# Single-core hybrid decoder layer: x blocks in rested places and loads untied, zeros on TensorE ahead of the first data, a residual sum between two side products, late forms' sums ten ticks on

## The chip, the core and the metric

The kernel runs on one core of a Trainium2 chip. The core has TensorE (PE, matmuls), VectorE (DVE), ScalarE (ACT), GpSimd (POOL) and SyncE (SP); SP and POOL issue the loads and stores, each from a queue of its own that is worked off in order. Each engine also runs its instructions in the order in which they stand in its own list, and waits at the first whose input is missing. The metric is the time of one execution in microseconds of device time.

## The reference

One layer on 512 tokens with 2048 columns, all in float32:

```python
h    = rmsnorm(x, attn_norm_g);  proj = h @ w_in          # 9216 columns: u, v, q, k, v_att, g_a, g_b
y_a  = chunked spatial gating of u, v                      # 8 groups, chunks of 128
y_b  = stick-breaking attention of q, k, v_att             # 8 heads of 128, strictly causal
x    = x + (sigmoid(g_a) * (y_a @ w_up_a) + sigmoid(g_b) * (y_b @ w_up_b)) @ w_o
hid  = rmsnorm(x, ffn_norm_g) @ w_ffn_in                   # 2 x 5632 columns, gate and up
x    = x + (silu(gate) * up) @ w_ffn_out
x    = x + sigmoid(rmsnorm(x, ple_norm_g) @ w_ple_gate) * (p @ w_ple)   # p: 512 x 256
```

## The kernel before

Everything lies transposed: columns on the 128 partitions, the 512 tokens along the free axis. x is eight blocks of 256 columns, each 128 x 1024 numbers. A float32 matrix is split into a high part that TensorE takes at its fast float32 rate and the rest (`split_into`: ACT writes the high part, DVE subtracts it), and a product is three matmuls: high by high, high by low, low by high (`mm3`, lines L268 to L270). Most products are done by Strassen's scheme on pairs of blocks: seven products in place of eight, of sums of the four quarters of each operand ("S" forms, L659); the rest are plain ("P"). What is prepared of an activation block is called a form: the gain of the norm by ACT (`gained`, L499), four sums by DVE (L512), and the splits (L263 by ACT, L264 by DVE). Weights go through three steps: they land in `wholes`, DVE adds sums (L363), ACT makes `whi` (L347), DVE makes `wlo` (L344); there are three places for `whi` and `wlo`. A finished unit is brought together by DVE from the PSUM banks (L702, L705).

Two arenas hold it all: `parts` for forms and `wholes`, 13200 columns for what lands. A place is taken "low" (the lowest hole), "high", "tight" (the smallest hole) or "rested" (the place that has been free longest). A place that is taken again makes the next load wait until everything that read it is done. Beside them there are two wide buffers, `out`, handed out in turn.

The program is traced by a planner. A counter, `clock`, ticks once per product of a pair of forms. At each tick the next form in the list `builds` goes a step on if its places fit (`fits`), up to three forms ahead may fetch their raw block early, and postponed steps that are due are put in. The instructions that a tick adds are kept behind the products already issued. Loads of weights and x are held in the order in which the code wrote them by `in_order`.

*The head.* The side product p @ w_ple comes in eight pairs of columns (`ple_pair`): the first three are done at the very start while x arrives, each ending in an ACT copy from PSUM to `out` (L830) and a store. Then the first three units of w_in are made plainly, block by block of x, while x arrives; their weights are `w_first`. `x_form(k)` loads x up to block k + 2, applies the gain, adds the block's squares to the first norm (`Norm.add`: ACT squares L901, DVE sums L905) and splits it.

*The end of w_o.* The product with w_o goes through eight blocks j; each ends with the residual's sum (`pr.onto`, L757) and its squares for the second norm. After the products of the last block `ple_pair` 3 and 4 stand ahead of that sum, 5, 6 and 7 after. The norm then sums squares over partitions by TensorE (L914), takes the power, builds four diagonal blocks on DVE (`diagonals`, L888) and spreads the row over the partitions with four matmuls of these diagonals (L930).

*The FFN.* 43 hidden units from w_ffn_in, whose results are stored to memory ("hid", 22 blocks); then w_ffn_out in three passes over the hidden blocks, the first two with five S forms ahead of three or two plain ones. S forms of hidden blocks and of x2 are `late_form`: they fetch the raw block early, and do their four sums in `plain_first` when they are built, ahead of the splits.

## Time and profile before

| | us |
|---|---|
| three runs, median | 2719.37 (2715.48 to 2728.74) |
| the profiled execution, its own time | 2723.71 |
| its span (first to last instruction) | 2721.8 |
| mean granted TensorE clock | 0.995 |
| PE busy | 2670.8 (98% of the span) |
| DVE busy | 2166.5 (80%) |
| ACT busy | 1357.0 (50%) |
| POOL busy | 392.8 (14%) |

In the chain of work that ended last, PE has 84%, DVE 6%, DMA 4%, ACT 3%. A row of a timeline below reads: start in us, duration in us, engine, line, operation, output <- input, and in brackets the engine's idle time ahead of it with what ended it. A row of the stages: the stretch, its length, and for each engine its busy time with the number of instructions, then the granted clock, the mean share of the DMA engines and what they moved in GB/s. Line numbers in the profile are those of the kernel before; the rows of the order after carry the changed kernel's own numbers.

### The profile page before, as it was taken

Reading aid. Unit: us, or ns where it says so; the run is one execution under the profiler, and the core shown is the slowest. Engines: PE = TensorE matmul, PEld = TensorE weight load, DVE = VectorE, ACT = ScalarE, POOL = GpSimd, SP = SyncE. Lnnn points to the kernel's source line nnn. Section 1 sums busy time; section 2 is a strip of 40 time slices with the busy share of each in tenths; the row PEclk is TensorE's granted clock in tenths of the full one; section 3 lists DMA queues with packets and bytes.
Section 4 is the critical chain, followed back from the end, with each engine's and each line's share of the span. In section 5 each row is a group of like instructions: output and inputs, shape, how many; then the busy total and the mean of one; then the engine's idle time right before and its main releaser. Section 6 shows DMA issues by size and latency. Waiting matters only on the chain.

```text
span 2721.8 us, 43177 instructions
## 1 busy us (share of the span) xinstructions
PE 2670.8 (98%) x15907; PEld 2358.2 (87%) x15907; DVE 2166.5 (80%) x3715; ACT 1357.0 (50%) x2143; POOL 392.8 (14%) x439
## 2 busy tenths in 40 slices
PE   6999999999999999999999999999999999999999
PEld 5888888888888889988888888888888998989898
DVE  6687878788888657678989898989899567688876
ACT  6565656564555334365444444444445344454543
POOL 0112121211220000001111111111110111101110
PEclk8999999999999999999999999999999999999999
DMA  5667677777776447667888888788886668788784
GB/s 175 165 169 181 177 178 178 175 182 193 175 182 220 135 137 223 196 200 188 209 221 201 208 197 207 200 204 202 203 203 194 171 175 247 203 250 233 253 223 135
DMA packets 303412, 528.88 MB, mean 194 GB/s; under 512 B 25696, under 2 KB 162912, under 8 KB 303200
## 3 DMA queue, kind: packets, MB, share of 16 engines
q1 hardware_dynamic: 242448, 425.70, 49.1%
q0 software_dynamic: 60752, 100.43, 23.1%
q8 instruction: 125, 2.05, 0.3%
q14 instruction: 87, 0.71, 0.1%
HBM read 478.84 MB, written 47.19 MB: 193 GB/s over the span
## 4 chain that ended last, share of the span: by engine, by line
PE 84%; DVE 6%; DMA 4%; ACT 3%; issue 2%; POOL 0%; SPq 0%; DVEq 0%; ACTq 0%; POOLq 0%
PE ps L659 38%; PE ps L268 13%; PE ps L270 13%; PE ps L269 13%; PE small L659 4%; DVE wlo L344 2%; ACT whi L347 1%; DMA wholes<-w_in 1%; DVE parts L264 1%; DVE wholes L512 1%; DVE out L705 1%; DVE wholes L705 1%; PE small L1090 1%; PE small L1048 1%; DVE wholes L363 1%
## 5 line engine op out<-in xcount | busy, mean ns | idle before, releaser
L347 ACT ACTIVATE whi<-wholes 128x512 fp32r<-128x512 f32 (+4 forms) x950 | 846.9, 916 | 845.2 <-DVE wholes L363 286.4
L659 PE MATMUL ps<-parts,whi 128*128 128x512 f32 x3384 | 1127.1, 397 | 3.0 <-DVE p L705 1.9
L344 DVE TENSOR_TENSOR wlo<-wholes,whi 128x512 fp32r<-128x512 f32 (+4 forms) x950 | 961.6, 1044 | 97.5 <-ACT whi L347 96.5
L268 PE MATMUL ps<-parts,whi 128*128 128x256 f32 (+1 forms) x2675 | 857.3, 323 | 28.6 <-ACT whi L347 23.1
L269 PE MATMUL ps<-parts,whi 128*128 128x256 f32 (+1 forms) x2640 | 856.3, 324 | 0.9 <-DVE parts L264 0.9
L270 PE MATMUL ps<-parts,wlo 128*128 128x256 f32 (+1 forms) x2640 | 854.9, 324 | 1.8 <-DVE wlo L344 1.8
L659 PEld LDWEIGHTS ps<-parts,wlo 128*128 128x128 f32 x3384 | 634.9, 188 | 141.0
L659 PE MATMUL ps<-parts,wlo 128*128 128x256 f32 x3384 | 667.5, 278 | 0.0
L268 PEld LDWEIGHTS ps<-parts,whi 128*128 128x128 f32 x2675 | 509.5, 191 | 75.0 <-ACT whi L347 25.2
L659 PEld LDWEIGHTS ps<-parts,whi 128*128 128x128 f32 x3384 | 542.7, 189 | 10.2 <-issue 3.9
L269 PEld LDWEIGHTS ps<-parts,whi 128*128 128x128 f32 x2640 | 502.9, 191 | 45.1 <-DVE parts L264 2.2
L270 PEld LDWEIGHTS ps<-parts,wlo 128*128 128x128 f32 x2640 | 502.8, 190 | 41.0 <-DVE wlo L344 2.4
L363 DVE TENSOR_TENSOR wholes<-wholes 128x256 f32<-128x256 f32 (+1 forms) x794 | 327.7, 413 | 21.1 <-DMA wholes<-w_ffn_out 3.0
L351 POOL DMA_DIRECT2D wholes<-w_ffn_in x172 | 149.7, 870 | 752.4 <-DVE wlo L344 219.2
L705 DVE TENSOR_TENSOR out<-out,ps 128x256 f32<-128x256 f32 x373 | 152.9, 420 | 127.4 <-ACT out L702 116.6
L351 POOL DMA_DIRECT2D wholes<-w_in x132 | 116.7, 884 | 637.9 <-DMA wholes<-w_in 294.2
L264 DVE TENSOR_TENSOR parts<-wholes,parts 128x1024 fp32r<-128x1024 f32 (+3 forms) x129 | 122.4, 962 | 19.1 <-ACT parts L263 18.9
L659 PE MATMUL small<-parts,whi 128*128 128x512 f32 x344 | 136.0, 395 | 0.0
L1359 ACT ACTIVATE out<-out 128x512 f32<-128x512 f32 x44 | 27.8, 632 | 195.2 <-DVE out L1358 195.2
L263 ACT ACTIVATE parts<-wholes 128x1024 fp32r<-128x1024 f32 (+3 forms) x129 | 105.8, 844 | 32.7 <-DMA wholes<-hid 11.1
L351 POOL DMA_DIRECT2D wholes<-w_ffn_out x56 | 56.9, 1015 | 397.9 <-DMA wholes<-w_ffn_out 146.4
L673 DVE TENSOR_TENSOR out<-out 128x256 f32<-128x256 f32 x36 | 15.3, 424 | 120.5 <-ACT out L670 120.5
(125 smaller groups left out, 1655.2 us busy)
## 6 DMA issues: line engine op xcount, KB each, us to landing
wholes<-w_ffn_in SPq DMA_DIRECT2D x172, 384.0 KB, 5.5
wholes<-w_in SPq DMA_DIRECT2D x132, 384.0 KB, 5.1
wholes<-w_ffn_in SPq DMA_DIRECT2D x172, 256.0 KB, 4.7
wholes<-w_ffn_in POOLq DMA_DIRECT2D x172, 256.0 KB, 5.2
wholes<-w_in SPq DMA_DIRECT2D x132, 256.0 KB, 4.1
wholes<-w_in POOLq DMA_DIRECT2D x132, 256.0 KB, 4.9
wholes<-x SPq DMA_DIRECT2D x32, 512.0 KB, 5.4
wholes<-w_ffn_out SPq DMA_DIRECT2D x31, 512.0 KB, 4.2
```

The source lines that it names most:

```text
L263: return (nc.scalar.activation(hi, src, AF.Copy), nc.vector.tensor_tensor(out=lo, in0=src, in1=hi.bitcast(F32), op=ALU.subtract))
L264: nc.vector.tensor_tensor(out=lo, in0=src, in1=hi.bitcast(F32), op=ALU.subtract))
L268: nc.tensor.matmul(ps[:, s], sh, mh[:, s], start=start, stop=False)
L269: nc.tensor.matmul(ps, sh, ml, start=False, stop=False)
L270: return nc.tensor.matmul(ps, sl, mh, start=False, stop=stop)
L344: in_turn(nc.vector.tensor_tensor(out=self.lo[:, blocks], in0=r, in1=h.bitcast(F32), op=ALU.subtract))
L347: in_turn(nc.scalar.activation(h, r, AF.Copy))
L351: nc.gpsimd.dma_start(out=raw[:, 3:5], in_=self.src[:, 1:3], accum_op=ALU.add)
L363: in_turn(nc.vector.tensor_tensor(out=o, in0=x, in1=y, op=ALU.add))
L659: i = nc.tensor.matmul(out, w, t, start=first and k == 0, stop=last and k == 1)
L705: in_turn(nc.vector.tensor_tensor(out=out, in0=x, in1=y, op=op))
L1359: nc.scalar.activation(g, g, AF.Silu)
```

## The change

- Ahead of everything five matmuls of zeros (128 x 256, float32) run on TensorE, into a bank that nobody reads. They need only a memset by DVE.
- p (`pT`) is loaded and split in two halves; its place is an ordinary one.
- The blocks of x are taken "rested" as far as the fourth (later ones "low"), so is the scaled copy in `x_form` as far as the third; `x_form(k)` loads up to block k, not k + 2. `in_order` is gone: loads of x and of weights have no order but that of SP's queue as the scheduler makes it.
- The three ple results of the head are stored by POOL's queue, later ones by SP's as before.
- At w_o's end the residual's sum stands between `ple_pair(3)` and `ple_pair(4)`.
- The second norm's row (and the others') is asked for two ticks later.
- A late form has its gain and its four sums done ahead of being built, ten ticks or more after its fetch (`sum_early`), if there is room for the sums and a spare block.
- How many spare blocks of 1024 columns that asks for (`spared`) is one, two from the start of the last pass, none once its last x1 block is loaded.

```diff
...
 PARTS = 16 * PLACE
 WHOLES = 13200
 FETCHED = 3
+WARM = 5
+LANDS = 10
 KEPT = 3
 HIDE = 2.0**99
 
...
             builds.popleft().step()
         for f in list(builds)[:FETCHED]:
             if f.fetches and f.early and f.ready():
-                if fits([(wholes, f.fetches, "low"), (wholes, 1024, "low")]):
+                if fits([(wholes, f.fetches, "low")] + spare_blocks()):
                     f.fetch()
                 break
+        any(f.sum_early() for f in list(builds)[:FETCHED])
         while waiting and waiting[0][0] <= clock[0]:
             heapq.heappop(waiting)[2]()
         for i in reversed(traced()):
...
                                          mybir.DependencyReason.DATA),
                     reason="in its place among the units")
 
+    spared = [1]
+
+    def spare_blocks():
+        return [(wholes, 1024, "low")] * spared[0]
+
     class Staged:
 
 
...
         spare[0] = sum(-1 for x in prepared if x.land.n < LANDING)
 
     chain = {}
-
-    def in_order(i):
-
-        if i.ins.engine in chain:
-            tc.add_manual_dep(
-                i.ins, chain[i.ins.engine],
-                mybir.DependencyInfo(mybir.DependencyClass.NoSync,
-                                     mybir.DependencyReason.DATA),
-                reason="in its place among the loads")
-        chain[i.ins.engine] = i.ins.name
 
     def in_turn(*instructions):
 
...
             landings.remove(self.land)
             raw = self.blocks(self.land.f())
             if kind == "P":
-                in_order(nc.sync.dma_start(out=raw, in_=src))
+                nc.sync.dma_start(out=raw, in_=src)
             else:
-                in_order(nc.sync.dma_start(out=raw[:, 3:5],
-                                           in_=src[:, 0:1].to_broadcast([P, 2, n * P])))
+                nc.sync.dma_start(out=raw[:, 3:5],
+                                  in_=src[:, 0:1].to_broadcast([P, 2, n * P]))
                 nc.sync.dma_start(out=raw[:, 0:3], in_=src[:, 1:4])
 
         def blocks(self, t, c=None):
...
             self.kind, self.places, self.ready = kind, sizes, ready
             self.blocks, self.at_plain, self.used = None, kind == "P", False
             self.src, self.fetches, self.raw, self.early = src, raw, None, False
+            self.late, self.gain, self.sums, self.since = False, None, None, None
 
         @property
         def sizes(self):
-            return self.places + [(wholes, self.fetches, "low")] * bool(self.fetches)
+            return (self.places + [(wholes, self.fetches, "low")] * bool(self.fetches)
+                    + SUMS * (self.late and self.sums is None))
 
         def fetch(self, block=None):
 
             if self.raw is None:
                 self.raw, self.fetches = block or self.src(), 0
+                self.since = clock[0]
             return self.raw
+
+        def scale(self):
+
+            if self.gain:
+                gained(self.raw.f(), self.raw.f(), *self.gain)
+                self.gain = None
+
+        def sum_early(self):
+
+            if not self.late or self.sums or self.since is None or clock[0] < self.since + LANDS:
+                return False
+            if self.gain:
+                self.scale()
+            elif fits(SUMS + spare_blocks()):
+                self.sums = sums_of(self.raw)
+            return True
 
         def get(self):
             if self in builds:
...
                                      AF.Copy, scale=gcol[:, gi + 2 * k + i : gi + 2 * k + i + 1])
                 for i in range(2)]
 
-    def plain_first(form, raw):
-
-
-        b, s, v = cut(raw.f()), take(768, "tight"), take(256, "tight")
-        t, x = cut(s.f()), form.operand()
+    SUMS = [(wholes, 768, "tight"), (wholes, 256, "tight")]
+
+    def sums_of(raw):
+
+        b, s, v = cut(raw.f()), *(take(n, how) for _, n, how in SUMS)
+        t = cut(s.f())
         for out, p, q, op in ((t[:, 0], b[:, 1], b[:, 0], ALU.subtract),
                               (v.f(), b[:, 1], b[:, 3], ALU.subtract),
                               (t[:, 1], t[:, 0], b[:, 3], ALU.subtract),
                               (t[:, 2], t[:, 1], b[:, 2], ALU.add)):
             nc.vector.tensor_tensor(out=out, in0=p, in1=q, op=op)
+        return s, v
+
+    def plain_first(form, raw):
+
+
+        s, v = form.sums or sums_of(raw)
+        b, t, x = cut(raw.f()), cut(s.f()), form.operand()
         split_into(x[:, 0:4, 0], x[:, 0:4, 1], b)
         give(raw)
         form.at_plain = True
...
         def steps(form):
             w = form.fetch()
             form.blocks = (parts.take(2 * PLACE, "place"),)
-            if gain:
-                gained(w.f(), w.f(), *gain)
-            yield
+            if not form.sums:
+                form.scale()
+                yield
             yield from plain_first(form, w)
             return form.operand()
 
-        return Form("S", steps, [(parts, 2 * PLACE, "place"), (wholes, 768, "tight"),
-                                 (wholes, 256, "tight")], ready, src, 1024)
+        f = Form("S", steps, [(parts, 2 * PLACE, "place")], ready, src, 1024)
+        f.late, f.gain = True, gain
+        return f
 
     def strassen_form(src, ready=always, gain=None, raw=PLACE):
 
...
     ps_p = []
 
     def ple_operands():
-        raw = load(pT)
+        raw = take(1024)
         hi, lo = parts.take(1024, "high"), parts.take(1024, "high")
-        split_into(hi.own(), lo.own(), raw.f())
+        for s in (slice(0, T), slice(T, 2 * T)):
+            nc.sync.dma_start(out=raw.f()[:, s], in_=pT[:, s])
+            split_into(hi.own()[:, s], lo.own()[:, s], raw.f()[:, s])
         give(raw)
         ps_p.extend((hi, lo))
 
...
                 mm3(ps, wh[:, s], wl[:, s], xh, xl, k == 0, k == 1)
             nc.scalar.activation(o[:, i * T : (i + 1) * T], ps, AF.Copy)
         d = tc.dram_tile([P, 1024], F32, name=nm("ple"))
-        nc.sync.dma_start(out=d, in_=o)
+        (nc.sync if planned else nc.gpsimd).dma_start(out=d, in_=o)
         ple_spill[j] = d
         slots.append(slot)
         tick()
...
     x_raw = []
 
     def load_x():
-        x_raw.append(take(1024))
-        in_order(nc.sync.dma_start(out=x_raw[-1].f(), in_=xT[len(x_raw) - 1]))
-
+        x_raw.append(take(1024, "rested" if len(x_raw) < KU - 4 else "low"))
+        nc.sync.dma_start(out=x_raw[-1].f(), in_=xT[len(x_raw) - 1])
+
+    idle, nothing = wide(), bank()
+    nc.vector.memset(idle[:, : T // 2], 0.0)
+    for _ in range(WARM):
+        nc.tensor.matmul(nothing[:, :T // 2], idle[:, :P], idle[:, :T // 2],
+                         start=True, stop=True)
     ple_operands()
     ple_pair(0, False)
     load_x()
...
             yield
             diags = diagonals(self.cols)
             yield
+            yield
+            yield
             ps = small_bank()
             for t in range(NT):
                 s = slice(t * P, (t + 1) * P)
...
 
     def x_form(k):
         def steps(form):
-            while len(x_raw) < min(k + 3, KU):
+            while len(x_raw) < min(k + 1, KU):
                 load_x()
             form.blocks = (parts.take(2 * PLACE, "place"),)
-            w = take(1024)
+            w = take(1024, "rested" if k < KU - 5 else "low")
             gained(w.f(), x_raw[k].f(), g_attn, k)
             norm1.add(x_raw[k])
             give(x_raw[k])
...
         pr = pair(ms, last=j == KU - 1)
         if j == KU - 1:
             ple_pair(3)
-            ple_pair(4)
         h = raw.popleft()
         pr.onto(h.f())
+        if j == KU - 1:
+            ple_pair(4)
         nc.sync.dma_start(out=spill["x1", j], in_=h.f())
         there.add(("x1", j))
         norm2.add(h)
...
         at += len(kinds)
         if c == len(PASSES) - 1:
             builds.extend(gs)
+            spared[0] = 2
         for j in range(KU):
             got = {}
 
             def fetch(*names, got=got, j=j):
                 for n in names:
                     got[n] = load(spill[n, j])
+                if "x1" in names and j == KU - 1:
+                    spared[0] = 0
 
             if c:
                 after(3, lambda f=fetch: f("sum"))
```

Three places show how it moves instructions. The first is SP's queue at the start: `pT` is p, `xT` a block of x, `ple` a stored side result, `w_first` the weights of the first three units. Before:

```order
L495 DMA wholes<-pT 128x1024
L327 DMA wholes<-w_ple 128x512
L853 DMA gcol<-gains 128x58
L847 DMA wholes<-xT 128x1024
L327 DMA wholes<-w_ple 128x512 x2
L327 DMA wholes<-w_first 128x512
L847 DMA wholes<-xT 128x1024
L832 DMA ple_107<-out_88 128x1024
L847 DMA wholes<-xT 128x1024
L832 DMA ple_158<-out_141 128x1024
L832 DMA ple_180<-out_163 128x1024
L847 DMA wholes<-xT 128x1024 x2
```

and with the change, the same queue from its first load:

```order
L841 DMA wholes<-pT 128x512 x2
L325 DMA wholes<-w_ple 128x512
L875 DMA wholes<-xT 128x1024
L886 DMA gcol<-gains 128x58
L325 DMA wholes<-w_ple 128x512 x2
L325 DMA wholes<-w_first 128x512
L875 DMA wholes<-xT 128x1024 x2
L325 DMA wholes<-w_first 128x512 x5
L327 DMA wholes<-w_in 128x2x256
```

The ple stores have left the queue; five blocks of x stood in it before the second group of `w_first` (the row after the last one above), now three, and the fourth comes after seven more loads of `w_first` and two of `w_in`.

The second place is ACT at the end of w_o. L830 (L858 with the change) is the copy of a ple result to `out`, L901 (L934) the Square of the last residual block into `out`, `whi` the weights' high part. Before:

```order
L347 ACTIVATE whi_76<-wholes 128x1024
L830 ACTIVATE out_10730<-ps_10731 128x512
L830 ACTIVATE out_10730<-ps_10739 128x512
L347 ACTIVATE whi_80<-wholes 128x1024
L901 ACTIVATE out_10759<-wholes 128x1024
L347 ACTIVATE whi_78<-wholes 128x1024
L830 ACTIVATE out_10766<-ps_10767 128x512
L830 ACTIVATE out_10766<-ps_10775 128x512
```

and with the change:

```order
L345 ACTIVATE whi_76<-wholes 128x1024
L858 ACTIVATE out_10747<-ps_10748 128x512
L858 ACTIVATE out_10747<-ps_10756 128x512
L934 ACTIVATE out_10773<-wholes 128x1024
L345 ACTIVATE whi_80<-wholes 128x1024
L271 ACTIVATE parts<-wholes 128x3x256
L858 ACTIVATE out_10780<-ps_10781 128x512
L858 ACTIVATE out_10780<-ps_10789 128x512
```

The two copies of ple 4 stay ahead; the Square has moved ahead of the next `whi`, and a split of a form has come in between. On PE, in the same stretch, the sums of squares over the partitions are row 6015 before and 6013 with the change, and the matmuls of the diagonals row 6073 before and 6086 with it. On DVE the last of the four diagonals then comes after a `wlo` of 128 x 1280.

The third place is DVE at the start of w_ffn_out's first pass. L512 (L530) are the sums of an S form, L264 (L272) its splits, L705 (L731) empties the PSUM banks of the last hidden unit. Before:

```order
L344 TENSOR_TENSOR wlo_79<-wholes,whi_78 128x1024
L512 TENSOR_TENSOR wholes<-wholes 128x256 x3
L264 TENSOR_TENSOR parts<-wholes,parts 128x4x256
L512 TENSOR_TENSOR wholes<-wholes 128x256 x4
L264 TENSOR_TENSOR parts<-wholes,parts 128x4x256
L512 TENSOR_TENSOR wholes<-wholes 128x256
L264 TENSOR_TENSOR parts<-wholes,parts 128x3x256
L512 TENSOR_TENSOR wholes<-wholes 128x256 x2
L264 TENSOR_TENSOR parts<-wholes,parts 128x4x256
L512 TENSOR_TENSOR wholes<-wholes 128x256
L264 TENSOR_TENSOR parts<-wholes,parts 128x3x256
L512 TENSOR_TENSOR wholes<-wholes 128x256
```

then the first L705; and with the change:

```order
L342 TENSOR_TENSOR wlo_79<-wholes,whi_78 128x1024
L272 TENSOR_TENSOR parts<-wholes,parts 128x4x256 x2
L272 TENSOR_TENSOR parts<-wholes,parts 128x3x256 x2
L530 TENSOR_TENSOR wholes<-wholes 128x256 x3
L272 TENSOR_TENSOR parts<-wholes,parts 128x4x256
L530 TENSOR_TENSOR wholes<-wholes 128x256
L731 TENSOR_TENSOR out_18713<-out_18713,ps_18588 128x256
```

Twelve sums stood ahead of the first L705 there; four do with the change. The other eight, of the first two hidden forms, now stand among the units of w_ffn_in.

## The prediction

> **What bounds the kernel now.** I read the page first (busy shares), then PE's waits, then a table by stage, and last the timelines of the places where PE stands still.
>
> ```profile
> span 2721.8 us, 43177 instructions
> PE 2670.8 (98%) x15907; PEld 2358.2 (87%) x15907; DVE 2166.5 (80%) x3715; ACT 1357.0 (50%) x2143; POOL 392.8 (14%) x439
> ```
> ```profile
> PE ps L268 <- ACT whi L347: 23.1, 6, 12.9
> PE small L930 <- DVE out L888: 4.6, 3, 2.3
> PE ps L268 <- ACT out L830: 2.8, 2, 1.5
> PE ps L268 <- DVE out L705: 2.4, 1, 2.4
> ```
> TensorE is the bound: 2721.8 - 2670.8 leaves 51.0 us in which it does nothing. The change adds or takes away no matmul of the layer, so all that can be won is those 51 us and the time in which PE runs at half speed. The waits (us in total, times, longest) say that one wait of 12.9 us is a quarter of the idle time. The stages say where the rest is:
>
> ```profile
> core 0: us, PE busy (x) PEld busy (x) DVE busy (x) ACT busy (x) POOL busy (x), PEclk, DMA share, GB/s
> 0.00:10.00 10.00, 3.93 (x9) 2.83 (x10) 2.14 (x5) 3.09 (x4) 0.95 (x7) 1.00 0.47 152
> 10.00:20.00 10.00, 8.86 (x37) 6.66 (x36) 3.69 (x6) 8.69 (x17) 0.00 (x0) 1.00 0.71 270
> 20.00:30.00 10.00, 1.15 (x6) 0.61 (x4) 8.96 (x18) 6.79 (x9) 0.00 (x0) 0.70 0.34 111
> 30.00:40.00 10.00, 5.94 (x19) 4.73 (x20) 8.82 (x15) 7.39 (x10) 0.00 (x0) 0.62 0.97 334
> 40.00:120.00 80.00, 75.25 (x365) 62.61 (x364) 49.56 (x89) 45.84 (x83) 8.46 (x9) 1.00 0.51 142
> ...
> 1235.00:2060.00 825.00, 825.00 (x4738) 719.85 (x4737) 743.53 (x1347) 390.62 (x553) 144.41 (x166) 1.00 0.82 204
> ```
> The first 120 us hold 24.9 us of PE's idle time, the end of w_o two more waits (2.3 on L888, 2.8 on L830), the start of ffn_out the one on L705; the FFN's first product, 1235 to 2060, has none. The change touches these three places with idle time and also the one without.
>
> **The head, part by part.** SP's queue and ACT, then PE:
>
> ```profile
> 6.78 0.33 SPq L847 DMA_DIRECT2D wholes<-xT  x1
> ...
> 25.55 3.51 SPq L847 DMA_DIRECT2D wholes<-xT  x2
> 29.12 1.37 SPq L327 DMA_DIRECT2D wholes<-w_first  x3
> ```
> ```profile
> 4.44 1.06 ACT L263 ACTIVATE parts<-wholes 128x1024 fp32r<-128x1024 f32 x1 [2.35 <-DMA wholes<-pT]
> ...
> 29.00 1.33 ACT L499 ACTIVATE wholes<-wholes,gcol 128x512 f32<-128x512 f32 x2 [3.18 <-DMA wholes<-xT]
> 30.24 1.04 ACT L901 ACTIVATE out<-wholes 128x1024 f32<-128x1024 f32 x1
> ```
> ```profile
> 6.07 0.80 PE L268 MATMUL ps<-parts,whi 128*128 128x512 f32 x1 [6.07 <-ACT whi L347]
> ...
> 34.06 0.79 PE L268 MATMUL ps<-parts,whi 128*128 128x512 f32 x1 [12.91 <-ACT whi L347]
> 34.65 0.63 PE L269 MATMUL ps<-parts,whi 128*128 128x512 f32 x1
> 35.08 0.63 PE L270 MATMUL ps<-parts,wlo 128*128 128x512 f32 x1
> ```
> SP issues its loads in one order. x's block 0 takes the place that pT lay in, so it goes out only at 6.78; blocks 3 and 4 take low places again and wait for them until 25.55, and the second group of weights, which has room, stands behind them until 29.12. They land some 4 us later, ACT makes whi of them, and PE, dry since 21.1, goes on at 34.06, for eight matmuls at half speed (starts 0.43 apart; below, at 2072, 0.23).
>
> The change puts pT (in halves), the first w_ple and x's block 0 into the queue without a wait, takes x into the places longest free, and drops the order between x and weights; the order of SP after has nine weight loads between the third block of x and the fourth. So the 12.91 us go. *Upper bound of the gain:* 12.91, the small waits of 10:20 (10.00 - 8.86 = 1.14), those of 40:120 (80.00 - 75.25 = 4.75), 0.2 because the first operand is ready a little sooner, and the slow clock, (9 + 8) matmuls of 0.2 = 3.4 and 0.2 for the first one: 22.6. *Lower bound:* PE's wait covered work. By 40 us ACT has done 3.09 + 8.69 + 6.79 + 7.39 = 25.96 us and DVE 23.61; ACT cannot start before pT lands at 4.44, so if all of this must still come first, the same point is reached no earlier than 4.44 + 25.96 = 30.4, a gain of 9.6. But two of the x forms were built ahead of need (three blocks ahead before, one now); each costs ACT 1.33 for the gain, 1.04 for the square and 1.06 for the split, 6.9 for two. Postponed, the bound is 23.5, a gain of 16.5. I choose **15**: nearest to that row, less some of the small waits that a PE fed hand to mouth will now have (in 40:120, with ACT at 57%, it lost 6%; 6% of 25 us is 1.5). The zeros are in this sum: PE is idle till 6.07 anyway, so five matmuls cost nothing as long as they end before the first weights are split; if they run 1 us over, 1 us is lost. What they save, nine slow matmuls, is 2.0. The three ple results move from SP's queue to POOL's, which is idle there (0.00 busy from 10 to 40).
>
> **The end of w_o.**
>
> ```profile
> 1200.62 1.22 DVE L757 TENSOR_TENSOR wholes<-wholes,out 128x1024 f32<-128x1024 f32 x1
> ```
> ```profile
> 1201.18 1.09 ACT L830 ACTIVATE out<-ps 128x512 f32<-128x512 f32 x2 [2.39 <-DMA ple<-out]
> ```
> ```profile
> 1228.23 1.47 PE L930 MATMUL small<-out,ones 128*128 128x128 f32 x8 [2.30 <-DVE out L888]
> 1229.35 0.77 PE L268 MATMUL ps<-parts,whi 128*128 128x512 f32 x1
> ```
> There are two wide "out" buffers. One is held by the residual of w_o until L757, the other by the ple result before, until its transfer has landed, so ple 4's copy waits to 1201.18 and PE loses 1.34 + 1.46 = 2.8 on PSUM banks. With the residual's add ahead of ple 4, its buffer is free near 1198 instead. But now the Square that follows in ACT's queue, with a whi copy right behind it, wants the next buffer, which the ple 3 transfer frees at the same 1201.18, and ple 5's copy waits for ple 4's transfer, issued near 1199. The waiting is handed on: I count 0, between 2.8 won and 2 lost. The row of norm 2 is asked for two ticks later: the order of PE has 73 instead of 58 rows between the sums of squares and it, 15 matmuls of 0.23 = 3.4 us, more than the stall of 2.30. Of that stall and six slow matmuls after it (1.2) some 0.5 stays, since DVE builds the fourth diagonal after a long split. **3** in all, 0 to 6.
>
> **The start of ffn_out.**
>
> ```profile
> 2074.73 0.42 DVE L512 TENSOR_TENSOR wholes<-wholes 128x256 f32<-128x256 f32 x1
> 2075.07 1.07 DVE L705 TENSOR_TENSOR out<-out,ps 128x256 f32<-128x256 f32 x3
> ```
> ```profile
> 2072.60 0.39 PE L659 MATMUL small<-parts,wlo 128*128 128x256 f32 x2
> 2072.83 0.40 PE L659 MATMUL small<-parts,whi 128*128 128x512 f32 x1
> 2075.62 0.77 PE L268 MATMUL ps<-parts,whi 128*128 128x512 f32 x1 [2.40 <-DVE out L705]
> 2076.19 0.63 PE L269 MATMUL ps<-parts,whi 128*128 128x512 f32 x1
> ```
> PE needs banks that DVE empties at 2075.07, after twelve sums (L512) and the splits of three forms. In the order after, eight of the twelve are gone from there; at 0.33 us a piece (starts 0.34 apart) that is 2.7 us, so L705 starts near 2072.4, and PE, dry from 2073.2, does not stop. 2.40 and seven slow matmuls (1.4) make 3.8; I take **3.5** (1 to 3.8), as one split there also waits for a place. The eight sums now stand in the FFN's first product. DVE has 825.00 - 743.53 = 81 us free there, so they cost nothing; without that cover 2.7.
>
> The clock has a rule to set against this. The trace closes the gate after 2.30 and 2.40 us of idling (starts 0.43 apart behind both). The Trainium skill, "TensorE: Matmul & The Clock Gate", section "What's actually happening", has the clock fall only after an idle window of about 3.4 us. By that rule the two later places would have lost no clock, and 2.6 us less would be won; the trace does not agree, so I keep the rows.
>
> **Sum.** 15 + 3 + 3.5 = 21.5 us. The profiled run took 2723.71, so 2702.2; the median of the three runs, 2719.37, is 4.3 lower, which gives 2697.9. I say **2700**.
>
> **The rivals.**
>
> *ACT takes over the head.* The x forms cannot be postponed enough, or a Square on ACT waits for a ple result that leaves by POOL, with the weights' copies queued behind it. For it: ACT was 8.69 busy of 10 at 10:20, with three such results under way. Against it: POOL's queue is empty, and the squares come later than the copies. The head then gives 9.6, one place more gives 2 to 4: 12.5 in all, 2709.
>
> *Only the head pays.* The two later waits are handed on (to ple 5's copy, to the split that waits for its place): 15, 2706.5. For it: both edits move a wait on a buffer or a queue that stays in use.
>
> *Everything goes.* Head 22, w_o 6, ffn_out 3.8: 32, 2691 by the profiled run, 2688 by the median, so 2689. Against it: ACT's 25.96 us.
>
> *Slower: the weights' lead in the FFN's first product.* The sums of two forms now lie in the arena of 13200 columns from the sixth unit or so to the end, and one later block is not fetched early: about one block of 1024 columns more is held, so weights may be asked for later in each of some 148 doubles.
>
> ```profile
> ACT whi L347 <- PE ps L659: 38.9, 34, 1.2
> ...
> ACT whi L347 <- DMA wholes<-w_ffn_in: 4.2, 2, 2.1
> ```
> For it: in 1700 to 2050 ACT already waits twice for w_ffn_in, and the DMA share is 0.82. Against it: 34 times it waits for PE instead, so the weights are there, and their landings have their own places. It decides from 0.15 us a double (22 us); at 0.3 it costs 44 and the time is 2742.
>
> *The zeros do nothing for the clock*, or PE cools before the weights come: 2.0 less, 2702, inside the forecast's range.
>
> **How the numbers follow.** Forecast 0.51 (own range 2694 to 2705), ACT in the head 0.20, only the head 0.15, everything 0.10, slower 0.04. From 2690 to 2712 the range holds the first three cases and a little of the fourth. Half a per cent, what a measurement here can tell from no change, is 13.6 us: faster means under 2705.8. That is 0.49 of the forecast, half of "only the head", all of "everything" and a third of "ACT": 0.73. The same: 0.23. Slower: 0.04.
>
> **What would show it.** Right: no wait over 3 us on PE in 10 to 100 us; no half-speed matmul after the first; the first product of x near 14.5; weights in SP's queue ahead of x; no wait of PE on L965's diagonals over 1 us; none on L731 at the start of ffn_out. Wrong: a PE wait of 4 us or more between 20 and 60 us whose releaser is ACT behind a ple transfer, or any idle time of PE where 1235 to 2060 stands now.

## The result, and the profile after

The changed kernel takes 2707.47 us (median of 16 runs, 2702.40 to 2714.11), the kernel before 2724.01 us (16 runs, 2715.48 to 2730.41). The ratio is 0.9942, 95% interval 0.9931 to 0.9952: 15.8 us faster, 13 to 19 with the interval. The forecast was 2700, from a sum of 21.5 us; the time lies in the range of 2690 to 2712, and three quarters of that sum came. One of the six runs of c2 below took 3185.07 us at a granted clock of 0.767 and is left out of its median.

The page of the kernel after, its span and the busy time of the engines:

```profile
span 2708.1 us, 43211 instructions
PE 2674.2 (99%) x15917; PEld 2359.8 (87%) x15917; DVE 2164.6 (80%) x3718; ACT 1355.6 (50%) x2145; POOL 392.0 (14%) x442
```

PE stands idle for 33.9 us instead of 51.0. Its waits after (line and releaser, us in total, times, longest):

```profile
PE ps L276 <- ACT whi L345: 5.1, 5, 1.8
PE ps L685 <- DVE p L731: 3.2, 5, 0.9
PE ps L278 <- DVE wlo L342: 3.2, 3, 1.4
PE ps L276 <- ACT out L858: 3.1, 1, 3.1
...
PE small L965 <- DVE out L921: 0.2, 1, 0.2
```

The row of 23.1 us with a longest of 12.9 is down to 5.1, the diagonals' row (L930, now L965) from 4.6 to 0.2, and the one on L705 (now L731) before ffn_out has gone. One row has grown: the wait on the copies of ple results (L830, now L858), 2.8 us in two pieces, is now 3.1 us in one.

Where the gain arose is read from places that both kernels pass. First the timeline of PE before: the first wait of the attention's `sp`, the sums of squares of the second norm, and a wait of 0.73 us inside the first pass of w_ffn_out.

```profile
141.04 0.33 PE L1078 MATMUL small<-sp,tri 128*128 128x128 f32 x1 [1.05 <-DVE sp L264]
...
1211.89 0.95 PE L914 MATMUL small<-ones,wholes 128*128 128x1 f32 x8
...
2089.47 0.39 PE L268 MATMUL ps<-parts,whi 128*128 128x256 f32 x1 [0.73 <-ACT whi L347]
```

and the same three after:

```profile
128.78 0.33 PE L1113 MATMUL small<-sp,tri 128*128 128x128 f32 x1 [2.57 <-DVE sp L272]
...
1204.65 0.95 PE L947 MATMUL small<-ones,wholes 128*128 128x1 f32 x8
...
2074.06 0.39 PE L276 MATMUL ps<-parts,whi 128*128 128x256 f32 x1 [0.73 <-ACT whi L345]
```

| us earlier than before | before | after | gained in the stretch |
|---|---|---|---|
| the attention's first `sp`, start of the wait (start less the wait) | 139.99 | 126.21 | 13.8 |
| sums of squares, end of w_o | 1211.89 | 1204.65 | -6.5 |
| inside ffn_out's first pass | 2089.47 | 2074.06 | 8.2 |
| end of the span | 2721.8 | 2708.1 | -1.7 |

So in these profiles the head and the stretch with the norm's row and the start of ffn_out gave 22.0, about what was forecast for the sum, and 8.2 were given back, most of it between the head and the end of w_o.

**The head.** SP's queue and PE after:

```profile
4.56 1.25 SPq L875 DMA_DIRECT2D wholes<-xT  x2
6.28 8.39 SPq L325 DMA_DIRECT2D wholes<-w_first  x5
```
```profile
1.26 3.86 PE L880 MATMUL ps<-out 128*128 128x256 f32 x10 [1.26 <-DVE out L878]
6.97 0.50 PE L276 MATMUL ps<-parts,whi 128*128 128x512 f32 x1 [1.85 <-ACT whi L345]
...
7.87 0.63 PE L277 MATMUL ps<-parts,whi 128*128 128x512 f32 x1
...
27.12 0.50 PE L276 MATMUL ps<-parts,whi 128*128 128x512 f32 x1 [1.76 <-ACT whi L345]
```

Weights stand in the queue from 6.28 on, and no wait of PE is over 2.6 us in the first 130 us. The wait at 27.12 has ACT behind it: a Square waits 1.63 us (to 24.54) for a ple result that leaves by POOL, with whi behind it. The zeros end at 5.12 (each matmul of zeros counts as two in the profile); the first weights come at 6.97, not sooner than before (6.07), and between 7.5 and 10.9 seven matmuls still run at half speed.

**The end of w_o.** ACT, then PE, after:

```profile
1191.90 1.06 ACT L934 ACTIVATE out<-wholes 128x1024 f32<-128x1024 f32 x1 [2.33 <-DMA ple<-out]
...
1195.66 1.09 ACT L858 ACTIVATE out<-ps 128x512 f32<-128x512 f32 x2 [1.01 <-DMA ple<-out]
```
```profile
1196.31 0.80 PE L276 MATMUL ps<-parts,whi 128*128 128x512 f32 x1 [3.14 <-ACT out L858]
1196.90 0.63 PE L277 MATMUL ps<-parts,whi 128*128 128x512 f32 x1
...
1202.02 0.52 PE L277 MATMUL ps<-parts,whi 128*128 128x512 f32 x1
```

The wait has been handed on as the prediction's working has it: the Square waits for ple 3's transfer, ple 5's copy for ple 4's. But now it is one wait of 3.14 us, and twelve matmuls at half speed (0.2 us each) behind it make it 5.6, twice the 2.8 before, at which the clock stayed up.

**The start of ffn_out.** DVE and PE after:

```profile
2060.77 0.41 DVE L530 TENSOR_TENSOR wholes<-wholes 128x256 f32<-128x256 f32 x1
2061.11 1.07 DVE L731 TENSOR_TENSOR out<-out,ps 128x256 f32<-128x256 f32 x3
```
```profile
2061.56 0.39 PE L685 MATMUL small<-parts,whi 128*128 128x512 f32 x1
2061.79 0.39 PE L276 MATMUL ps<-parts,whi 128*128 128x512 f32 x1
```

L731 starts before PE has finished its unit; PE goes straight on, at full speed.

### The profile page after: what moved, and what is told of

Read it like the earlier page. It is cut to its first block, busy times and chain, and to the rows that moved or that the text cites. A ratio compares the mean times of both kernels' runs of the same rounds, so it can differ in the third digit from the quotient of the medians.

```text
span 2708.1 us, 43211 instructions
## 1 busy us (share of the span) xinstructions
PE 2674.2 (99%) x15917; PEld 2359.8 (87%) x15917; DVE 2164.6 (80%) x3718; ACT 1355.6 (50%) x2145; POOL 392.0 (14%) x442
## 4 chain that ended last, share of the span: by engine, by line
PE 81%; DVE 8%; DMA 5%; ACT 3%; issue 2%; POOL 0%; SPq 0%; DVEq 0%; ACTq 0%; POOLq 0%
PE ps L685 38%; PE ps L276 12%; PE ps L278 12%; PE ps L277 12%; PE small L685 4%; DVE wlo L342 3%; DVE parts L272 1%; DMA wholes<-w_in 1%; DVE wholes L731 1%; ACT whi L345 1%; DVE out L731 1%; DMA wholes<-hid 1%; PE small L1125 1%; PE small L1083 1%; DMA wholes<-x 1%
## 5 line engine op out<-in xcount | busy, mean ns | idle before, releaser
L731 DVE TENSOR_TENSOR out<-out,ps 128x256 f32<-128x256 f32 x373 | 152.6, 420 | 126.1 <-ACT out L728 115.4
L272 DVE TENSOR_TENSOR parts<-wholes,parts 128x1024 fp32r<-128x1024 f32 (+4 forms) x131 | 122.4, 949 | 13.9 <-ACT parts L271 13.9
L271 ACT ACTIVATE parts<-wholes 128x1024 fp32r<-128x1024 f32 (+4 forms) x131 | 105.7, 834 | 36.3 <-DMA wholes<-hid 13.2
```

The costliest lines, as they stand in the source:

```text
L271: return (nc.scalar.activation(hi, src, AF.Copy), nc.vector.tensor_tensor(out=lo, in0=src, in1=hi.bitcast(F32), op=ALU.subtract))
L272: nc.vector.tensor_tensor(out=lo, in0=src, in1=hi.bitcast(F32), op=ALU.subtract))
L731: in_turn(nc.vector.tensor_tensor(out=out, in0=x, in1=y, op=op))
```

## The experiments

All are made from the changed kernel. Times are medians, ratios are against the kernel before on the same chip; an interval of 0.001 is 2.7 us. The changed kernel itself was timed only with the result above; beside the three groups of experiments the kernel before took 2722.67, 2722.37 and 2721.47 us, up to 2.5 less than there. A difference from the changed kernel of under some 3 us is therefore not read as one.

**e9: both halves of the edit on x's loads undone.** In the diffs of this section a line with - is the changed kernel's. `in_order` is also back around the weights' loads, and the scaled copy of x in a low place.

```diff
-        x_raw.append(take(1024, "rested" if len(x_raw) < KU - 4 else "low"))
-        nc.sync.dma_start(out=x_raw[-1].f(), in_=xT[len(x_raw) - 1])
+        x_raw.append(take(1024))
+        in_order(nc.sync.dma_start(out=x_raw[-1].f(), in_=xT[len(x_raw) - 1]))
-            while len(x_raw) < min(k + 1, KU):
+            while len(x_raw) < min(k + 3, KU):
```

> The changed kernel with both halves of the edit on x's loads undone: x in low places, loaded up to block k + 2, and the order between loads of x and of weights is back. Zeros, the halves of p, the ple stores by POOL and everything behind the head stay. If the loads are what the head's gain comes from: a PE wait of 10 to 14 us for a whi copy comes back between 20 and 36 us, and the time is 11 to 16 us above the changed kernel's. If the halves of p, the zeros and the stores by POOL carry the gain: no wait over 4 us there, and less than 6 us above it.

Measured: 2721.44 us, ratio 0.9988 (0.9979 to 0.9998), 14.0 above the changed kernel. Its waits of PE in the first 110 us:

```profile
PE ps L276 <- ACT whi L355: 18.7, 5, 14.3
```

The long wait is back, and with it all but 3 us of the gain. The zeros, the halves of p and the stores by POOL do not carry the head; the loads do.

**e7: the tie alone.** x stays in rested places and is loaded up to block k; only `in_order` is back.

```diff
-        nc.sync.dma_start(out=x_raw[-1].f(), in_=xT[len(x_raw) - 1])
+        in_order(nc.sync.dma_start(out=x_raw[-1].f(), in_=xT[len(x_raw) - 1]))
...
-                nc.sync.dma_start(out=raw, in_=src)
+                in_order(nc.sync.dma_start(out=raw, in_=src))
```

> The changed kernel with the order between loads back, x still in rested places and loaded up to block k. If it is the tie that held the weights (the reading of the prediction: the second group of weights has room and stands behind x): a PE wait of 5 us or more between 20 and 40 us, 5 to 13 us above the changed kernel. If the tie only hurt because x's low places were not free: no wait over 3 us, within 3 us of the changed kernel.

Measured: 2721.14 us, 0.9993 (0.9983 to 1.0003): the same loss, 13.7. SP's queue and the waits of PE in the first 110 us:

```profile
22.52 0.33 SPq L885 DMA_DIRECT2D wholes<-xT  x1
22.94 1.33 SPq L335 DMA_DIRECT2D wholes<-w_first  x3
36.42 0.33 SPq L885 DMA_DIRECT2D wholes<-xT  x1
36.80 1.37 SPq L335 DMA_DIRECT2D wholes<-w_first  x3
```
```profile
PE ps L276 <- ACT whi L355: 11.5, 7, 4.0
```

The longest wait is only 4.0 us, where 5 or more was expected; the loss now comes in pieces. Each x holds the three weight loads behind it: SP issues one group at 22.94 and the next not before 36.80. The reading "the tie only hurts with low places" falls.

**e8: the places alone.** Low places and three blocks ahead again, no tie.

```diff
-            while len(x_raw) < min(k + 1, KU):
+            while len(x_raw) < min(k + 3, KU):
-            w = take(1024, "rested" if k < KU - 5 else "low")
+            w = take(1024)
```

> The changed kernel with x back in low places and loaded up to block k + 2, without the tie. If the tie held the weights: they go out ahead of x, no wait over 3 us for a whi copy, x's block 0 comes some 4 us later (it waits for p's place again), 0 to 5 us above the changed kernel. If the places are the cause: a wait of 8 us or more, whose end is a landing of x, and 8 to 14 us above it.

Measured: 2707.01 us, 0.9940 (0.9924 to 0.9957), no difference from the changed kernel; its longest wait for whi in the first 110 us is 3.0 us. e9 is this kernel with the tie, and e7 the changed one with it: both times the tie costs 14 us. The rested places are worth nothing that can be measured.

**e1 and e2: no zeros, and eight of them.** In e1 the memset and the matmuls of zeros are left out; e2 is this line:

```diff
-WARM = 5
+WARM = 8
```

> The changed kernel without the five matmuls of zeros. The prediction put their worth at 2.0 us (nine slow matmuls saved). The profile of the changed kernel shows eight slow ones after the zeros all the same, behind a pause of 1.85 us between the last zero and the first weights. If the zeros are worth only the difference: 0.2 to 1 us slower than the changed kernel, nine to twelve slow matmuls from the first one on, and every wait behind them the same. If they carry the head: 2 us or more slower.

> The changed kernel with eight matmuls of zeros in place of five. In most profiles five end near 5.5 us, the first weights come at 6.0 to 6.4 and the clock rises 0.3 to 1.4 us later. If the pause behind the zeros is what costs the clock: no slow matmul of the layer in the first 12 us, 0 to 1 us gained less what the zeros run over the first weights. If the zeros run over (they took 0.8 us each): the first matmul of the layer begins 1 to 2 us later, and the time is 0 to 2 us above the changed kernel.

Measured: without zeros 2709.39 us, 0.9946 (0.9932 to 0.9961); with eight 2704.88 us, 0.9935 (0.9918 to 0.9952), runs of 2704.18 to 2705.84. PE's first rows without zeros, then with eight:

```profile
7.37 0.79 PE L276 MATMUL ps<-parts,whi 128*128 128x512 f32 x1 [7.37 <-ACT whi L345]
7.97 0.63 PE L277 MATMUL ps<-parts,whi 128*128 128x512 f32 x1
```
```profile
1.26 6.37 PE L880 MATMUL ps<-out 128*128 128x256 f32 x16 [1.26 <-DVE out L878]
7.27 0.58 PE L276 MATMUL ps<-parts,whi 128*128 128x512 f32 x1
7.69 0.40 PE L277 MATMUL ps<-parts,whi 128*128 128x512 f32 x1
```

Eight zeros reach the first weights without a pause, push them back to 7.27 (5.9 to 6.4 in the ten profiles with five besides the changed kernel's), and no later matmul of the first 27 us is slow. The medians go the way that was expected, by 1.9 and 2.6 us, but the intervals overlap: neither step is shown by the times. In the changed kernel's own profile the pause of 1.85 us behind the zeros cost most of what they were for; in the ten other profiles with five zeros the pause was at most 0.64 us and at most three matmuls behind it were slow.

**e6: the head's ple results by SP's queue.**

```diff
-        (nc.sync if planned else nc.gpsimd).dma_start(out=d, in_=o)
+        nc.sync.dma_start(out=d, in_=o)
```

> The changed kernel with the three ple results of the head stored by SP's queue again. If a store in SP's queue holds up the loads behind it: loads of w_first go out 2 us or more later between 10 and 22 us, a PE wait of 2 to 5 us there, 1 to 5 us above the changed kernel. If the wait of ACT's Square for the POOL store (1.63 us in the changed kernel, PE 1.76 behind it) weighs more: that wait shrinks, and the time is 0 to 2 us below.

Measured: 2706.95 us, 0.9944 (0.9923 to 0.9965), no difference. The Square's wait of 1.63 us is gone, and a load of w_first goes out at 16.59 behind two stores that took SP from 14.58; no PE wait over 1.4 us follows in the first 110 us. So POOL's queue shows neither use nor harm in the times.

**e3, e5, e12: the end of w_o.** e3 puts the residual's sum behind ple 3 and 4 again, e5 takes the two ticks back, e12 does both.

```diff
             ple_pair(3)
+            ple_pair(4)
         h = raw.popleft()
         pr.onto(h.f())
-        if j == KU - 1:
-            ple_pair(4)
...
             diags = diagonals(self.cols)
             yield
-            yield
-            yield
```

> The changed kernel with the residual's sum of the last block behind ple 3 and ple 4 again, as before the change. If moving the sum only handed the wait on and made it one longer one (the profile of the changed kernel: one wait of 3.14 us and thirteen matmuls at half speed, 5.9 us, where there were two waits of 2.80 us in all): the two waits of 1.3 to 1.5 us on the PSUM banks come back without slow matmuls, and the stretch from the last product of w_o to the sums of squares is 2 to 3 us shorter than in the changed kernel's profile; the time is 0 to 3 us below it. If the moved sum helps: a stretch 1 us longer or more, and 1 to 3 us above it.

> The changed kernel with the norms' rows asked for as early as before (two ticks sooner). If these two ticks cover the diagonals, as the prediction has it: the wait of PE on the diagonals comes back at the second norm (1.5 to 2.5 us, six to eight slow matmuls if it is over 2.2) and the time is 2 to 5 us above the changed kernel; at the first norm, in the head, another 1 to 2 us. If the wait was there only because ple 4 and the residual came late: less than 1 us of it, and no difference.

> The changed kernel with both edits at w_o's end undone: the residual's sum behind ple 3 and ple 4, and the norms' rows asked for two ticks sooner. With one of the two undone no wait for the second norm's diagonals was left (runs e3 and e5). If either edit covers that wait alone: here it comes back, 1.5 to 2.5 us with up to seven slow matmuls, 2 to 4 us from the sums of squares to the row on top of the other runs. If neither does, and the wait went with the other edits (loads, early sums): no wait over 1 us here.

Measured: e3 2708.39 us, 0.9953 (0.9936 to 0.9970); e5 2711.17, 0.9958 (0.9942 to 0.9975); e12 2713.15, 0.9962 (0.9947 to 0.9977). PE in e3, and then in e12:

```profile
1189.98 0.50 PE L276 MATMUL ps<-parts,whi 128*128 128x512 f32 x1 [1.69 <-ACT out L858]
1193.89 0.50 PE L276 MATMUL ps<-parts,whi 128*128 128x512 f32 x1 [0.90 <-ACT out L858]
```
```profile
1214.86 1.76 PE L963 MATMUL small<-out,ones 128*128 128x128 f32 x8 [2.75 <-DVE out L921]
```

In e3 the two shorter waits are back, 2.6 us and no slow matmul behind them. From the first matmul on `sp` in the attention to the sums of squares the three profiles with the sum behind ple 4 take 1072.6 to 1074.2 us (e3, e12 and the run c2 below; 1072.2 before), the nine with it between and ple results in the wide buffers, 1073.1 to 1078.8, 1075.5 in the mean. The moved sum costs some 2 us there in the mean, though the two groups overlap: in eight of the nine the clock fell behind its one long wait, in none of the three behind the two short ones. The wait on the diagonals, on the other hand, is in neither e3 nor e5 but comes back in e12, with 2.75 us and five slow matmuls. Either edit covers it alone, and the second one brings nothing more at this wait. So the two ticks are not needed for it beside the moved sum. e5's time is all the same 3.7 us above the changed kernel, where it was expected if they were; its profile has the loss in another place: from inside ffn_out's first pass to the sums of squares of the last norm it takes 472.0 us (467.9 in the changed kernel), with a wait of 3.0 us for the split of a form.

**e4: late sums when the form is built.**

```diff
-        any(f.sum_early() for f in list(builds)[:FETCHED])
```

> The changed kernel without the early sums: late forms do gain and sums when they are built, as before. If the prediction is right about the start of w_ffn_out: a PE wait of 2.0 to 2.8 us on the emptying of the PSUM banks with seven or eight slow matmuls comes back, 3.5 to 4 us above the changed kernel. If the wait went because the change moved a raw block's load: no wait there, no difference. At the start of the last pass and of w_gate less than 1.5 us either way.

Measured: 2711.24 us, 0.9964 (0.9952 to 0.9976), 3.8 above the changed kernel. PE at the start of ffn_out:

```profile
2057.84 0.54 PE L275 MATMUL ps<-parts,whi 128*128 128x512 f32 x1 [2.40 <-DVE out L730]
2058.18 0.63 PE L276 MATMUL ps<-parts,whi 128*128 128x512 f32 x1
```

The same wait of 2.40 us with its slow matmuls is back, and from the sums of squares to the place inside ffn_out's first pass the profile takes 873.4 us, 4.0 more than the changed kernel's. This term stands by itself.

**c3 and c2: towards a faster one.** c3 takes e8's loads and copies ple 3 and 4 to blocks of their own, so that no copy and no Square waits for a transfer; c2 takes e8's loads and e3's order.

```diff
-        o = wide()
+        own = take(1024, "rested") if planned and j in (3, 4) else None
+        o = own.f() if own else wide()
```

> The changed kernel with x in low places and loaded up to block k + 2 (untied, the run e8), and with ple 3 and 4 at the end of w_o copied to blocks of their own in the arena of what lands instead of the two wide buffers. If the wait on ACT for a wide buffer, held by a ple transfer under way, is what PE waits for at w_o's end: no wait over 1 us there and no slow matmuls, 2 to 6 us below the changed kernel. If the banks wait for something else (the whi copies, the weights' landing): a wait of 1.5 us or more stays and the time is within 2 us of the changed kernel's.

> The changed kernel without the two edits that the runs so far show no use of: x in low places and loaded up to block k + 2 (untied), and the residual's sum behind ple 3 and 4. If these two only move waits about: 2705 to 2709, no difference from the changed kernel by the interval. If the short wait at w_o's end (0 to 13 slow matmuls) is worth its 3 us and the load order of run e8 another 1: 2703 to 2705.

Measured: c3 2708.75 us, 0.9948 (0.9929 to 0.9967); c2 2707.31, 0.9940 (0.9924 to 0.9956). In c3 no wait on a copy is left at w_o's end, and the sums of squares come 1069.3 us after `sp`, the shortest of all; but PE then waits 1.48 us for the split of a form, and the row of the norm comes 2.2 us later behind the sums than in the changed kernel (19.5 us against 17.3). So a wide buffer is what PE waits for there, but taking the wait away did not move the time, against the 2 to 6 us that were expected. c2 equals the changed kernel. None of the twelve beats it by more than the intervals; e2, with 2.6 us, comes nearest, and against the kernel before timed beside it, it gains no more than the changed kernel does (16.6 and 16.5).

## Why the prediction was right or wrong

- **The 12.91 us and their cause: right.** Weights behind x in SP's queue: e7 against the changed kernel, and e9 against e8, show that it is the order. The term was 15, the profiles give 13.8, and e9 against the changed kernel 14.0. The bound from below (ACT must do the same work first, 9.6) and from above (22.6) held it; the choice by ACT's postponed work was good to 1.2. The other profiles with untied loads reach `sp` at 121.5 to 127.3 us: one execution says this term to about 3 us.
- **The zeros: their size came out, the way did not.** The first weights were to come a little sooner; they come 5.9 to 6.4 us from the start in ten profiles, where 6.07 was before, and 0.9 later than that in the changed kernel's own, where the pause undid the warm clock. 2.0 was said, 1.9 is the difference of the medians, within their noise, so that the two agree is luck. Two signs of the forecast failed with it: seven half-speed matmuls came after the first, and the first product of x (after the 36 matmuls of the three ple results) began at 16.99, not near 14.5.
- **w_o, "I count 0, between 2.8 won and 2 lost": wrong in size.** The hand-over was seen, and the next wait named (ple 5's copy). That the two short waits would become one of 3.14, long enough to slow the clock for twelve matmuls, was not: -2.8, outside its bounds. That is the changed kernel's profile; in the nine with this order the one wait is 2.0 to 3.1 us, and the slow spell behind it lasts for none, one or two steps of the clock (the last section).
- **w_o, the norm's row: the sum right, the cause only in part.** 3.0 was given to the two ticks. The stall went, with its slow matmuls, and e3 shows that the ticks alone do it, as forecast; but e5 and e12 show that the moved sum does it too. The edit that pays there is either one, and the moved sum has the cost above beside it.
- **ffn_out: right.** 3.5 said; 3.8 by the medians of e4, and of the 8.2 in the table some 4 are this one. L731 comes a quarter of a microsecond ahead of PE's need, so it was near.
- **"So they cost nothing" in the FFN's first product: right.** PE is busy 825.00 of 825.00 us from 1235 to 2060 after, too, and DVE has 747.70 where it had 743.53. The rival on the weights' lead is out.
- **What was missed.** From `sp` to the end of w_o 6.5 us were lost, of which 2.8 at the waits above. Through the attention and the gates the rest goes, in waits of 0.2 to 0.9 us and between them, where the order of PE and DVE is the same in both kernels. The same stretch without w_o differs by 3 us among the untied profiles (648.4 to 651.6), and the kernel before has but one profile (647.8): so most of this is of the size by which one execution differs from the next. The end, from inside ffn_out's first pass, is 632.3 us before, 634.0 after and 631.5 to 639.2 in the other twelve, longer in eleven of them. Something there costs 2 to 4 us. Most of it is idle time of PE up to the last norm: 3.8 us before, 4.7 after, up to 8.6 in the others (e1), mostly in waits for `wlo` and for the split of a form. It is not the early sums (e4 has 637.2). With the loads tied again the end is 631.5 (e7, the shortest) and 635.9 (e9), and neither waits more than 0.2 us for such a split there; so the untied weights may have a part in it, but two profiles do not show it. The spare blocks were not tried, and the cause stays open.
- **Adding up.** Undone one by one, the loads, w_o, the sums and the zeros are worth 14.0, 5.7, 3.8 and 1.9, 25.4 in all; together they gave 15.8, and e9, which keeps all but the loads, is only 3.3 (0.5 to 5.7) faster than before. Each difference of two medians is uncertain by some 3 us, and the stretch that got longer is in nearly every one of them, so no exact split is claimed. The base moved too: the forecast started from 2723.71 and 2719.37, and sixteen runs put the kernel before at 2724.01. From there the sum of 21.5 gives 2702.5, so 5.0 us were missed.

The mechanism of the likeliest case was right in the head and at the start of ffn_out, but its own range, 2694 to 2705, was missed: the time lies in the wider range of 2690 to 2712 because that also holds the times of two rivals whose stories did not happen. Of these, "only the head pays" came closest (2706.5), by another way: the later places paid, and others took it back. That much is luck.

## What to carry to other kernels

Loads that nothing forces into one order should not be tied: one load that waits for its place holds everything behind it in the queue, and it did so even when the places were the best to be had. When two short waits at a shared buffer are merged into one, look at what the longer one does to the clock, not only at the sum. And before two edits are stacked against one stall, try each alone: here either was enough.

## What the runs showed of the hardware

By the length of a wait alone the fall of the clock can't be told: it fell behind 2.09 us at w_o in e7 and not behind 2.03 us there in e8, nor behind 2.35 us in e7's head. The granted clock of the profiles brings order into this. In each of the fourteen it changes only at moments that lie whole steps of 3.41 us apart. Below are four such steps at the end of w_o after the change, then three in e7's head around its wait of 4.00 us (37.72 to 41.72); a row has the step, its length, PE's busy time, the granted clock, the share of the DMA engines and their GB/s.

```profile
1192.04:1195.45 3.41, 1.13 (x5) 1.00 0.95 312
1195.45:1198.87 3.42, 2.56 (x6) 0.50 0.72 283
1198.87:1202.28 3.41, 3.41 (x9) 0.50 0.86 202
1202.28:1205.69 3.41, 3.41 (x20) 1.00 1.00 279
```
```profile
36.22:39.64 3.42, 1.50 (x7) 1.00 0.61 201
39.64:43.05 3.41, 1.33 (x5) 1.00 0.54 183
43.05:46.47 3.42, 3.42 (x10) 0.50 0.01 2
```

What counts is PE's idle time within one step. In all fourteen profiles a full-speed step was followed by one at half clock whenever it was 1.93 us or more (e5's head; 2.28 in the first row above), and where the rest of the step was full matmuls it never did at 1.92 us or less (the first row of e7). Where small matmuls, or in one step the zeros, stood beside the idle time, it fell from 1.33 us on, though not every time. A half-speed step was followed by a full-speed one when PE was idle for at most 0.38 us of it, and by another slow one from 0.85 us on; only a step with the 128x1 matmuls of a norm (e9) was followed by a slow one without that. So a wait costs more or less by where the steps cut it: the 4.00 us in e7 fall into two steps and cost one slow step, the 3.14 us at w_o reach 0.85 us into the slow step and cost two, and the two short waits there before the change left 1.1 and 1.3 us in their steps and cost none.

The Trainium skill ("TensorE: Matmul & The Clock Gate", "What's actually happening") has a window that runs freely, so that the moment varies; these rows agree with that. The idle time of about 3.4 us that it names is more than was needed here. Zeros count as work for this: in e2 the clock rose at 6.64 us, when PE had done nothing else, and in e1, without zeros, at 11.32.
